# A masked softmax: SyncE waits for a ScalarE half tile before its first store

## Chip, cores, metric

One core of a Trainium2 chip. The metric is the device time in microseconds (us). All runs used here are at a granted clock of 1.0.

## The reference

```python
x: (16, 8, 256, 256) float32, lengths: 16 integers from 128 to 255
for b in range(16):
    masked = x[b, :, :, :lengths[b]]
    e = exp(masked - max(masked, axis=-1))
    result[b, :, :, :lengths[b]] = e / sum(e, axis=-1)     # the rest stays 0
```

The kernel leaves out the row maximum, which the drawn data allow. Every run reported here gave a correct result.

## The kernel before

A tile is one batch element: 2048 rows as 128 partitions x 16 rows x 256 columns, 2 MB. There are eight slots for tiles. SyncE loads tiles 0 to 3 whole and stores everything; GpSimd loads tiles 4 to 15, only as wide as the length asks; VectorE masks and divides; ScalarE computes exp and row sums, half a tile at a time.

```python
for h in range(2):                                   # SyncE: tile 0 in halves
    nc.sync.dma_start(out=xt[:, 0, s], in_=x_f[0, :, s]).then_inc(s_ld[h], 16)
for b in range(1, ahead):                            # tiles 1 to 3 (ahead = 4)
    nc.sync.dma_start(out=xt[:, b], in_=x_f[b]).then_inc(s_ld[b + 1], 16)
for b in range(batch):                               # stores
    s_b = s_st[b % 2]
    for s in parts(b):                               # tile 0: one part
        nc.sync.wait_ge(s_out, 2 * b + (s.stop - 1) // half + 1)
        if b >= 2 and s.start == 0:
            nc.sync.wait_ge(s_b, 64 * (b // 2 + 1))
        nc.sync.dma_start(out=out_f[b, :, s, :], in_=xt[:, b % slots, s, :]
            ).then_inc(s_b, 16 * ((s.stop - s.start) // quarter))
# ... GpSimd
nc.gpsimd.wait_ge(s_ld[ahead - 1], 16)               # tile 2 has landed
with nc.Fori(0, (batch - ahead) // 2, 1, engines=[POOL]) as q:
    # ... waits for the slot from the second round on, then the load of one tile
# ... VectorE: s_min counts masked halves, s_out divided halves
# ... ScalarE
with nc.Fori(0, 2 * batch, 1, engines=[ACT]) as i:
    nc.scalar.wait_ge(s_min, i + 1)
    for j in range(half):                            # 8 row groups
        ins = nc.scalar.activation(out=e, in_=e, func=EXP, accum_out=...)
    ins.then_inc(s_exp, 1)
```

The softmax here doesn't subtract the row's maximum and nothing guards it: scores larger than these inputs give would overflow.

## Time and profile before

| | before |
|---|---|
| time, median of 3 runs (range) | 156.89 us (156.85 to 157.22) |
| span of the profiled run | 155.3 us |
| bytes moved | 62.08 MB, 400 GB/s over the span |
| busiest engine | VectorE, 74% |
| first store issued | 18.86 us |
| tile 3 landed | 25.0 us |

The transfers bound the kernel: the page shows the DMA engines busy 0.9 or more in 38 of 40 slices, and DMA is 77% of the chain that ended last. The one stretch in which they run far below their usual rate, apart from the first and the last slice, is 20.5 to 25 us; it is called "the dip" below. The prediction shows the lines for it. Beside the views the text uses the trace's single records of DMA packets (queue, start, duration, size). Each transfer of SyncE leaves 16 records of 4 bytes (656 for the 41 transfers of the kernel before). Each is read here as the end of one of 16 parallel parts of SyncE's queue, and such a part is called a ring; that there are such parts is my reading of these records. A transfer is called "in the rings" from its issue to its landing. "Excess" is the time that packets took beyond the usual duration of their size, summed over the slower ones and divided by 16 engines. A slow stretch is said to begin when its first slow packet is overdue, that is at this packet's start plus the usual 0.61 us of a 16 KB packet.

### The profile page before, as it was taken

How to read it: one execution, taken by the hardware profiler on the slowest of the kernel's cores; microseconds unless marked ns; L12 is line 12 of the kernel's file. 1: busy time of each engine (PE TensorE's matmuls, PEld its weight loads, DVE VectorE, ACT ScalarE, POOL GpSimd, SP SyncE). 2: the span in 40 equal slices, each digit the busy share in tenths (PEclk: the TensorE clock that was granted, in tenths of full speed). 3: DMA queues.
4: the chain of work that ended last, by engine and by line, in shares of the span. 5: the costliest groups of instructions: out<-in, count | busy, mean ns of one | idle time of the engine just before them, and what ended most of it. 6: DMA issues, size and time to landing. Idle time of an engine off the chain costs nothing.

```text
span 155.3 us, 1316 instructions
## 1 busy us (share of the span) xinstructions
PE 0.2 (0%) x1; PEld 0.1 (0%) x1; DVE 115.6 (74%) x84; ACT 105.2 (68%) x514; POOL 19.0 (12%) x25
## 2 busy tenths in 40 slices
PE   0000000000000000000000000000000000000000
PEld 0000000000000000000000000000000000000000
DVE  1249999951999697997969696969698639796600
ACT  3087799992492978869595959596886906959100
POOL 4910031000220020200211020202000000000000
DMA  4999999999999999999999999999999999999991
GB/s 127 426 443 422 443 304 398 419 411 442 412 410 390 415 411 419 406 415 417 402 423 410 414 411 405 417 417 416 413 425 410 423 436 441 414 443 426 420 426 65
DMA packets 9988, 62.08 MB, mean 400 GB/s; under 512 B 850, under 2 KB 946, under 8 KB 6274
## 3 DMA queue, kind: packets, MB, share of 16 engines
q1 hardware_dynamic: 5904, 41.95, 65.7%
q0 software_dynamic: 4080, 20.12, 32.0%
q14 instruction: 2, 0.02, 0.0%
q10 hardware_dynamic: 2, 0.00, 0.0%
HBM read 28.51 MB, written 33.55 MB: 400 GB/s over the span
## 4 chain that ended last, share of the span: by engine, by line
DMA 77%; issue 7%; DVE 3%; ACT 3%; POOLq 3%; SPq 1%; ACTq 0%; POOL 0%; DVEq 0%
DMA xt<-in_x_dram 77%; ACT xt L252 3%; DVE xt L195 2%; DVE xt L222 1%; POOLq L99 1%; POOLq L135 1%; POOLq L130 1%; SPq L109 1%; ACTq L252 0%; POOL xt L130 0%; SPq L111 0%; POOLq L157 0%; DVE inv_sum L219 0%; POOLq L153 0%; POOLq L159 0%
## 5 line engine op out<-in xcount | busy, mean ns | idle before, releaser
L252 ACT ACTIVATE xt<-xt x256 | 102.4, 401 | 37.5 <-DVE xt L195 37.5
L222 DVE TENSOR_TENSOR xt<-xt,inv_sum 128x2048 f32<-128x2048 f32 x32 | 73.4, 2292 | 1.1
L252 ACT ACTIVATION_READ_ACCUMULATOR xt<-xt x256 | 47.8, 187 | 0.0
L195 DVE SCALAR_TENSOR_TENSOR xt<-down,len_s,xt 128x2048 f32<-128x2048 f32 (+1 forms) x17 | 37.8, 2222 | 13.3 <-DMA xt<-in_x_dram 13.2
L130 POOL DMA_DIRECT2D xt<-in_x_dram x12 | 12.8, 1064 | 95.6 <-issue 53.0
L219 DVE RECIPROCAL inv_sum<-row_sum 128x8 f32<-128x8 f32 x32 | 6.4, 199 | 14.4 <-ACT xt L252 14.4
L149 POOL MEMSET xt<- 128x1536 f32 x4 | 5.3, 1386 | 1.3 <-DVE len_s L186 1.3
L244 ACT ACT_TABLE_LOAD x1 | 1.3, 1283 | 1.6 <-SPq L79 1.6
L178 DVE TENSOR_SCALAR down<-iota_i 128x256 f32<-128x256 int32 x1 | 0.3, 298 | 1.6 <-POOL iota_i L141 1.6
L183 DVE CAST len_b<-word 1x16 bf16<-1x16 int32 x1 | 0.2, 161 | 0.5 <-DMA word<-in_lengths_dram 0.5
L186 DVE TENSOR_SCALAR len_s<-len_f 128x16 f32<-128x16 f32 x1 | 0.2, 175 | 0.4 <-PE len_f L165 0.4
L141 POOL IOTA iota_i<- 128x256 int32 x1 | 0.3, 332 | 0.6 <-SPq L79 0.6
L146 POOL MEMSET seed<- 1x1 f32 x2 | 0.3, 162 | 0.0
L244 ACT ACTIVATE warm<-const-float32-0.0 128x1 f32<-128x1 f32 x1 | 0.2, 203 | 0.0
L144 POOL MEMSET ones<- 1x128 bf16 x1 | 0.2, 194 | 0.0
L165 PE MATMUL len_f<-len_b,ones 1*128 1x16 bf16 x1 | 0.2, 168 | 2.8 <-DVE len_b L183 2.8
L270 POOL MEMSET const-float32-0.0<- 128x1 f32 x1 | 0.1, 98 | 0.3 <-issue 0.3
L165 PEld LDWEIGHTS len_f<-len_b,ones 1*128 1x128 bf16 x1 | 0.1, 97 | 2.7 <-POOL ones L144 2.7
L270 POOL MEMSET const-float32-1.0<- 128x1 f32 x1 | 0.1, 98 | 0.0
L270 POOL MEMSET const-bfloat16-1.0<- 128x1 bf16 x1 | 0.1, 98 | 0.0
L270 POOL MEMSET const-uint8-127<- 128x1 uint8 x1 | 0.1, 98 | 0.0
L270 POOL BASE_LOAD x1 | 0.0, 17 | 0.1
## 6 DMA issues: line engine op xcount, KB each, us to landing
out_dram<-xt SPq DMA_DIRECT2D x19, 1024.0 KB
out_dram<-xt SPq DMA_DIRECT2D x14, 512.0 KB
xt<-in_x_dram SPq DMA_DIRECT2D x3, 2048.0 KB, 16.2
out_dram<-xt SPq DMA_DIRECT2D x3, 2048.0 KB
xt<-in_x_dram POOLq DMA_DIRECT2D x3, 1728.0 KB, 17.0
xt<-in_x_dram POOLq DMA_DIRECT2D x2, 2048.0 KB, 18.9
xt<-in_x_dram POOLq DMA_DIRECT2D x2, 1600.0 KB, 17.2
xt<-in_x_dram POOLq DMA_DIRECT2D x2, 1280.0 KB, 14.5
```

The costliest lines, as they stand in the source:

```text
L99: return nc.values_load(at, engines=[engine], skip_runtime_bounds_check_because="compared with constants, never an address",)
L109: nc.sync.dma_start(out=xt[:, 0, s], in_=x_f[0, :, s]).then_inc(s_ld[h], 16)
L130: nc.gpsimd.dma_start(out=xt[:, slot, :, :w], in_=x_n[:, n, :, :w]).then_inc(s_sw[par], 16)
L135: with nc.gpsimd.If(v <= ws[m]):
L149: nc.gpsimd.memset(xt[:, b, :, low:], 0.0).then_inc(s_fill, 1)
L165: nc.tensor.matmul(len_f, lhsT=ones, rhs=len_b, start=True, stop=True).then_inc(s_lenf, 1)
L195: return nc.vector.scalar_tensor_tensor(out=t, in0=down[:, None, lo:hi].to_broadcast([P, s.stop - s.start, hi - lo]), scalar=len_s[:, b : ...
L219: step(nc.vector.reciprocal(out=inv_sum[:, b, s], in_=row_sum[:, b, s]))
L222: nc.vector.tensor_tensor(out=t, in0=t, in1=inv_sum[:, b, s, None].to_broadcast([P, half, seq_k]), op=ALU.mult,).then_inc(s_out, 1)
L244: nc.scalar.activation(out=warm, in_=nc.const_aps.tensor(0.0, (P, 1), F32), func=EXP)
L252: ins = nc.scalar.activation(out=e, in_=e, func=EXP, accum_out=sum_h[:, bass.ds(i, 1), j])
L270: nc = _bacc.Bacc("TRN2", target_bir_lowering=False, num_devices=1)
```

## The change

The first store is issued when tile 0 is divided, at 18.86 us, while tile 3's load is still in flight. The change holds it back until ScalarE has done the first half of tile 1, about a microsecond later. The intent, it seems, is to let tile 3's load pass undisturbed.

```diff
         for b in range(1, ahead):
             nc.sync.dma_start(out=xt[:, b], in_=x_f[b]).then_inc(s_ld[b + 1], 16)
+
+        nc.sync.wait_ge(s_exp, 3)
         for b in range(batch):
             s_b = s_st[b % 2]
```

## The prediction

> **What bounds the kernel now.** I read four views in this order: the page, the chain of waits of SyncE's queue, the busy time by stretches around the first store, and the timeline of single engines there. The page first.
>
> ```profile
> span 155.3 us, 1316 instructions
> PE 0.2 (0%) x1; PEld 0.1 (0%) x1; DVE 115.6 (74%) x84; ACT 105.2 (68%) x514; POOL 19.0 (12%) x25
> DMA  4999999999999999999999999999999999999991
> GB/s 127 426 443 422 443 304 398 419 411 442 412 410 390 415 411 419 406 415 417 402 423 410 414 411 405 417 417 416 413 425 410 423 436 441 414 443 426 420 426 65
> HBM read 28.51 MB, written 33.55 MB: 400 GB/s over the span
> DMA 77%; issue 7%; DVE 3%; ACT 3%; POOLq 3%; SPq 1%; ACTq 0%; POOL 0%; DVEq 0%
> ```
>
> The DMA line is 9 in every slice but the first and the last, and no compute engine is over 74% busy: the 62 MB of transfers bound this kernel (9988 packets, 62.08 MB by the page), and 77% of the chain that ended last is DMA. The GB/s line says how evenly: a first slice that starts empty, a last one that drains, some 390 to 443 between, and one exception, slice six (19.4 to 23.3 us) with 304. That slice is where the change acts, so I cut it up.
>
> ```profile
> 14.00:17.00 3.00, 0.00 (x0) 0.00 (x0) 2.97 (x4) 1.08 (x6) 0.00 (x0) 1.00 1.01 431
> 20.00:20.90 0.90, 0.00 (x0) 0.00 (x0) 0.90 (x1) 0.90 (x5) 0.00 (x0) 1.00 1.02 382
> 20.90:23.20 2.30, 0.00 (x0) 0.00 (x0) 2.27 (x3) 2.30 (x13) 1.30 (x1) 1.00 0.93 235
> 23.20:25.00 1.80, 0.00 (x0) 0.00 (x0) 1.77 (x3) 1.80 (x10) 0.56 (x1) 1.00 0.97 382
> 25.00:26.20 1.20, 0.00 (x0) 0.00 (x0) 1.20 (x2) 1.20 (x8) 0.00 (x0) 1.00 1.02 437
> ```
>
> The last two columns are the DMA share and GB/s. The share stays at 0.93 or more: the engines are not idle in the dip, their packets take longer. The single packet records of the trace agree: 16 KB packets take 611 ns each before and after, and 0.9 to 1.7 us between 20.9 and 23.2. The dip costs (431-235) x 2.3 us + (431-382) x 1.8 us + (431-382) x 0.9 us = 583 KB, at 431 GB/s 1.35 us. Adding up the excess of each packet over the usual time of its size gives 1.1 us. So about 1.1 to 1.35 us of the 156.9 are lost here. All other excess in the trace is 0.5 us at the very first packets.
>
> Now who does what around it, from the timelines of the single engines (start, duration):
>
> ```profile
> 18.86 26.07 SPq L118 DMA_DIRECT2D out_dram<-xt  x8
> 16.54 2.29 DVE L222 TENSOR_TENSOR xt<-xt,inv_sum 128x2048 f32<-128x2048 f32 x1
> 19.45 0.40 ACT L252 ACTIVATE xt<-xt  x1
> 19.76 0.19 ACT L252 ACTIVATION_READ_ACCUMULATOR xt<-xt  x1
> 20.94 1.30 POOL L130 DMA_DIRECT2D xt<-in_x_dram  x1 [12.42 <-issue]
> 24.29 0.56 POOL L130 DMA_DIRECT2D xt<-in_x_dram  x1 [2.05 <-issue]
> ```
>
> And when the early loads landed: a piece of the chain (start, duration; GpSimd's wait for tile 2 ends there), and the landing times of SyncE's three whole-tile loads.
>
> ```profile
> 2.51 16.19 DMA xt<-in_x_dram
> ...
> DMA to landing us min/median/max: 11.8/16.2/21.8
> ```
>
> The first store is issued at 18.86, right after VectorE ends tile 0's second division at 16.54 + 2.29 = 18.83. At that moment the loads of tiles 0 to 2 have just landed (2.51 + 16.19 = 18.70), and tile 3's 2 MB are in the rings: its load, issued last at 3.26, took 21.8 us to land, so it landed at 25.0.
>
> [...]the rings' end-of-transfer records for tile 3 lie at 23.2 to 24.7 us, the store's packets follow directly, and its issue had come 4.3 us before the first of them. [...]here GpSimd's packets first appear at 26.3, 5.3 us after its instruction. [...]undisturbed stretches here have 431[...].[...]
>
> **The change, part by part.** It adds one wait on SyncE, before the loop of stores, and removes nothing. Its count of 3 is reached when ScalarE ends the eighth row group of tile 1's first half: that activation starts at 19.45 and its accumulator is read from 19.76 for 0.19, so 19.95. With the 0.03 us that the store now takes from VectorE's end to issue, it goes in at about 19.98, against 18.86: 1.1 us later. The wait for VectorE has then been over for 1.1 us and costs nothing more.
>
> What does this delay touch? From issue (1.13) to its first packet record (2.14) the first load took 1.0 us[...]. The earliest ring is through with tile 3 at 23.2; without any dip it would be 23.2 - 1.0 = about 22.2. So 1.2 us of slack are left without the dip, and 2.2 with it: no ring runs dry. The bytes, the packet sizes, and the order (tile 3's load, store 0, store 1, GpSimd's loads beside them) are the same. The second store is issued at 23.75, when its own data are ready, over 3 us after the delayed first one, so SyncE doesn't pile up. Store 0 should land when it landed before, at about 31.7 us (the wait on it ends there), and so tile 2's store and GpSimd's reload of slot 0 keep their times. Sum: +1.1 us of issue, 0 us of path, 0 us of span. At the end SyncE still waits 6.4 us for stores alone, with the DMA at 401 to 434 GB/s up to 151: the last stores leave at the rate of the queue.
>
> **The rivals.**
> First, the early store causes the dip: [...]the delay lets more of tile 3 pass at full rate. For it: the dip stands between the first issue of a store and its first packet, and the change was presumably made for this. Against it: slowing begins at once on most engines, between 20.93 and 20.99, two us after the issue, and no later store issue shows such a thing (25.0 to 26.2 has 437, with a store issued at 23.75). If true, the dip shrinks or goes: up to 1.35 us less, 155.5 to 156.6.
> Second, GpSimd causes it: its first transfer instruction starts at 20.94, to 0.05 us where the packets begin to slow, and it is the longest of the twelve (1.30 against a median of 1.15). Against it: the other eleven leave no dip, so it would have to be a cost of the first one alone. GpSimd waits for tile 2's load, not for SyncE's store, so the dip stays and the time stays at 156.9. I hold this for likelier, 3 to 1.
> Third, the delay goes through in full: a bubble between tile 3 and store 0, or a later store 0 that holds slot 0 and GpSimd's reload. Then +1.1 us, 158.0. The slack of 2.2 us speaks against it.
> Fourth, the order between the two queues tips: with the store 1.1 us later, GpSimd's first packets might come in before part of store 0. They came at 26.3 and store 0 would have begun by 23.2 to 24.7, so only a dip that changes shape could do this; it would move tile 4 forward and store 0 back by well under 1 us, with the same bytes in all. Compute has room: ScalarE idles 37.5 us for VectorE, and VectorE 13.2 us for loads.
>
> **Range and chances.** Three parts in four for no change (156.9), one in four, less a little for the third rival, for a gain of around 0.6 to 1.2 us: the mean is 156.7 to 156.8, and I say 156.8. The three runs of before spread over 0.4 us. The low end is the first rival nearly whole, 155.9; the high end is half of the third plus spread, 157.5. A verdict of faster needs 3.1 us, more than twice the whole dip; slower needs 3.1 us too, nearly three times the delay. Faster 0.015, same 0.97, slower 0.015.
>
> **What would show each step.** In the changed profile the first store's issue should stand at 19.9 to 20.1. The GB/s line should again have one slice near 300 at 19.4 to 23.3, with the slow packets beginning at GpSimd's first transfer, about 20.9. Tile 3 should land at about 25.0 (21.8 us after issue), store 0 near 31.7, and GpSimd's second group of loads at the same places, 39.6 and 45.7 within half a us. If instead slice six is at 400 or more and tile 3 lands near 23.7, the first rival was right and the span is a microsecond shorter. If the DMA share drops below 0.9 near 23 us, there was a bubble after all. If the dip moves by 1.1 us with the store and keeps its size, the store causes it but the delay only shifts it. I would be wrong altogether if the time left 155.5 to 158.0: then something chaotic in the interleaving of the two queues is at work that I have not seen.

The forecast's sum came to +1.1 us of issue, 0 us of path and 0 us of span, from 156.9; with the rivals weighed in, to 156.8. No term of the sum is cut. What is cut are statements on the hardware that no trace or run of this case shows: in what order the rings and the queues are served, a highest rate (with the conclusion that nothing but the dip could be gained), a reason to suspect GpSimd, and what becomes of a store between its issue and its first packet. In place of the last: the slack of 1.2 and 2.2 us is 22.2 and 23.2 less 21.0. That 21.0, when the store is taken to be ready, is my estimate: the issue at 19.98 plus the 1.0 us that the first load took from issue (1.13) to first packet (2.14). The first rival uses the same 1.0 us: it has the store disturb the loads in flight when it arrives, about 1 us after 18.86.

## The result

| | before | changed |
|---|---|---|
| time, median of 4 runs each | 156.91 us (156.85 to 157.22) | 156.49 us (156.29 to 156.66) |
| ratio, 95% interval | | 0.9968 (0.9951 to 0.9986) |
| span of the profiled run | 155.3 us | 155.0 us |
| tile 3 landed | 25.0 us | 23.7 us |
| packet excess, 20 to 26 us | 1.11 us | 0.54 us |

A ratio is the mean time of one kernel's runs over that of the other's runs of the same rounds, so it is not quite the ratio of the medians. All outputs are right.

The page of the changed kernel, GB/s in 40 slices:

```profile
GB/s 110 427 457 410 440 376 422 401 408 440 412 409 392 403 410 420 409 415 414 407 422 406 419 405 411 415 412 424 410 420 412 428 439 427 412 450 423 395 425 85
```

Slice six has 376 in place of 304; the other slices are as before, within the scatter of a slice that holds only a few hundred packets.

The changed kernel by stretches (length, busy times of the engines, granted clock, DMA share, GB/s):

```profile
20.00:20.90 0.90, 0.00 (x0) 0.00 (x0) 0.90 (x1) 0.90 (x7) 0.17 (x1) 1.00 1.02 437
20.90:23.20 2.30, 0.00 (x0) 0.00 (x0) 2.27 (x3) 2.30 (x13) 1.12 (x1) 1.00 0.99 349
23.20:25.00 1.80, 0.00 (x0) 0.00 (x0) 1.77 (x3) 1.80 (x11) 0.56 (x1) 1.00 1.01 401
```

Against 382, 235 and 382 of before: the dip is about half as deep. The share of 0.99 to 1.02 shows no bubble for the later store.

The timeline of SyncE's queue in the changed kernel (start, duration of the merged row):

```profile
19.76 8.05 SPq L120 DMA_DIRECT2D out_dram<-xt  x4
```

Its timeline of GpSimd:

```profile
20.73 1.29 POOL L132 DMA_DIRECT2D xt<-in_x_dram  x1 [12.36 <-issue]
```

And the landing times of SyncE's three whole-tile loads in it:

```profile
DMA to landing us min/median/max: 11.5/16.0/20.5
```

The store is issued at 19.76. In this run everything on ScalarE stands 0.2 us earlier than in the run of before (the first activation of tile 1 starts at 16.43, not 16.64), so the delay that the wait makes is 1.1 us, as worked out. GpSimd's first transfer starts at 20.73. But by the packet records the first packet is overdue at 21.66, not at 20.7: the slow packets no longer begin where GpSimd begins. Tile 3, issued at 3.19, lands 20.5 us later, at 23.7. Two more signs moved that the prediction had unmoved: the slowest ring ends store 0 at 29.5 us in place of 31.2, and GpSimd's second group of loads starts at 38.55 and 44.71 in place of 39.57 and 45.74.

So the dip seemed to depend on the store, and the cause that the prediction preferred was in doubt at once.

### The profile page after: what moved, and what is told of

Its sections match the earlier page's. It is cut to its first block, busy times and chain, and to the rows that moved or that the text cites. A ratio compares the mean times of both kernels' runs of the same rounds, so it can differ in the third digit from the quotient of the medians.

```text
span 155.0 us, 1317 instructions
## 1 busy us (share of the span) xinstructions
PE 0.2 (0%) x1; PEld 0.1 (0%) x1; DVE 115.8 (75%) x84; ACT 105.2 (68%) x514; POOL 19.0 (12%) x25
## 4 chain that ended last, share of the span: by engine, by line
DMA 74%; DVE 6%; issue 6%; ACT 4%; POOLq 2%; SPq 1%; ACTq 1%; DVEq 0%
DMA xt<-in_x_dram 65%; DMA out_dram<-xt 10%; ACT xt L254 4%; DVE xt L197 3%; DVE xt L224 3%; ACTq L254 1%; SPq L109 1%; POOLq L132 0%; POOLq L137 0%; SPq L120 0%; POOLq L99 0%; DVE inv_sum L221 0%; SPq L111 0%; POOLq L159 0%; POOLq L155 0%
## 6 DMA issues: line engine op xcount, KB each, us to landing
xt<-in_x_dram POOLq DMA_DIRECT2D x2, 2048.0 KB, 18.5
```

## The experiments

**Theories.** *Store*: the first store, standing in the rings behind the loads, slows the packets ahead of it. *GpSimd*: its first transfer slows whatever is in flight. *Chance*: the gain of 0.3% is a difference between builds and nothing else.

### GpSimd moved away: e1_pool_after_tile3

```diff
-        nc.gpsimd.wait_ge(s_ld[ahead - 1], 16)
+        nc.gpsimd.wait_ge(s_ld[ahead], 16)
```

> The kernel before, with GpSimd waiting for tile 3's load instead of tile 2's before its first transfer, so that no GpSimd transfer is issued until about 24 us; the store stays at 18.9. If the early store makes the dip: still about 235 GB/s between 20.9 and 23.2, tile 3 lands near 25.0. If GpSimd's first transfer makes it: 420 GB/s or more there, tile 3 lands near 23.7, and whatever the first transfer costs comes after 24 us. The time itself may rise, since GpSimd's loads come some 4 to 5 us later: I expect 156.5 to 158 under either theory, so it is the stretch that decides.

157.73 us, 1.0055 of before (1.003 to 1.0081). The timeline of GpSimd in this run:

```profile
27.20 1.29 POOL L130 DMA_DIRECT2D xt<-in_x_dram  x1 [18.83 <-issue]
```

The dip's stretch in this run (columns as before):

```profile
20.50:23.50 3.00, 0.00 (x0) 0.00 (x0) 2.97 (x4) 3.00 (x16) 0.00 (x0) 1.00 0.97 289
```

The same stretch of the kernel before:

```profile
20.50:23.50 3.00, 0.00 (x0) 0.00 (x0) 2.97 (x3) 3.00 (x17) 1.30 (x1) 1.00 1.00 289
```

GpSimd does nothing between 20.5 and 23.5 (0.00 in the fifth column), its first transfer is 6.3 us later, and the rate is the same 289 GB/s. The first packet is overdue at 20.45, 1.8 us after the store's issue at 18.68. GpSimd is not needed for the dip. Its theory falls. The kernel got slower at its end: GpSimd's loads come later, and the last store is issued at 150.2 in place of 147.0.

### GpSimd earlier: e4_pool_early

```diff
-        nc.gpsimd.wait_ge(s_ld[ahead - 1], 16)
+        nc.gpsimd.wait_ge(s_ld[ahead - 2], 16)
```

> The kernel before, with GpSimd waiting for tile 1's load instead of tile 2's, so that its first transfer is issued near 16 us, 3 us before the first store. If GpSimd's first transfer makes the dip: slow packets from about 16 us, and none at 20.9. If the early store does: full rate at 16 to 18 and the dip about two us after the store's issue as before. Time 155.5 to 157.5: the same bytes, but tile 4 moves ahead of part of tile 3.

156.88 us, 1.0004 (0.998 to 1.0028). GpSimd's first transfer started at 15.98. The packets between 14 and 20 us have an excess of 0.06 us, those between 20 and 26 of 1.25. The stretch 20.5 to 23.5 has 314 GB/s, now with GpSimd's small packets, the first at 20.42, among the loads. The dip didn't move with GpSimd's instruction. As its packets lie in the dip here, the clean test is e1.

### No store in the rings until the loads have ended: e2_store_after_tile3

```diff
+        nc.sync.wait_ge(s_ld[ahead], 16)
         for b in range(batch):
```

> The kernel before, with SyncE waiting for tile 3's load to land before the first store is issued, so that no store is in the rings while loads are in flight. If the early store makes the dip: 420 GB/s or more until the loads end, which is then at about 22.2 to 23.2; tile 3 lands near 23.6, followed by a bubble of 1 to 1.5 us[...]. If GpSimd's first transfer makes it: packets slow down from about 20.9 all the same, tile 3 lands near 25.0, and then the bubble. Time: 156.5 to 157 under the first theory, 157.5 to 158.5 under the second.

157.95 us, 1.0082 (1.0059 to 1.0105). By stretches:

```profile
14.00:22.00 8.00, 0.00 (x0) 0.00 (x0) 7.82 (x7) 6.08 (x31) 1.11 (x1) 1.00 1.01 434
22.00:24.00 2.00, 0.00 (x0) 0.00 (x0) 1.97 (x3) 2.00 (x11) 0.74 (x2) 1.00 0.63 127
24.00:28.00 4.00, 0.00 (x0) 0.00 (x0) 4.00 (x2) 4.00 (x21) 0.00 (x0) 1.00 0.94 289
```

The timeline of SyncE's queue, with the first store:

```profile
23.71 1.22 SPq L119 DMA_DIRECT2D out_dram<-xt  x2
```

With no store behind them the loads run at 434 GB/s up to 22 us; by the packet records the rings finish tile 3 at 22.2 to 23.1 and not one of its packets takes over 700 ns, though GpSimd's first transfer started at 20.89. A gap follows (share 0.63). GpSimd's first packet comes at 22.89, and that of the store, issued at 23.71, only at 27.32. So from 23.1 until then all packets are GpSimd's, and many are slow in turn (excess 0.87 us between 20 and 26, 0.83 between 26 and 40), about 0.6 us of it before 24, when the store had hardly been issued. Here, then, the loads ahead were not slow without an early store, but the next stream started slowly without one. The store theory's mark is there; its time of 156.5 to 157 was wrong by a microsecond, probably because it had not allowed for GpSimd's slow packets beside the gap.

### The instruction without the delay: e3_wait_already_met, r2_wait_already_met

```diff
-        nc.sync.wait_ge(s_exp, 3)        # the changed kernel
+        nc.sync.wait_ge(s_exp, 2)
```

> The changed kernel with the count 2 in place of 3: the new wait is met at about 15 us, long before the wait for VectorE, so the instruction is there and the delay is not. Both theories of the dip say 156.9, first store at 18.9, the dip at 235 GB/s as before. If the gain of the change comes from the instruction itself or from chance of the build, this one shows it too, near 156.5.

157.19 us, 1.0033 (1.0008 to 1.0057). The store was issued at 18.98, and the stretch 20.5 to 23.5 has 289 GB/s: the full dip, as expected. But the time was 0.3% above before, not equal to it. That is as much as the change itself had gained, so single ratios of this size can't be taken for the effect. I ran both kernels again, on one chip:

> The control with count 2 again: the instruction without the delay. If the gain is the delay's, this one is 0.2 to 0.5 per cent slower than the changed kernel on the same chip, so 1.000 to 1.003 of before, with the full dip. If builds differ by chance only, no order between the two is expected.

> The changed kernel a third time, beside its control (next run) on one chip. Earlier: 0.9968 and 0.9987 of before. Expected 0.997 to 0.999, the dip again half as large as before (about 0.5 us of packet excess between 20 and 26 us against 1.0 to 1.1).

The changed kernel took 156.47 us, 0.9996 of before (0.9974 to 1.0017), the control 156.87, 1.0015 (0.9992 to 1.0037). The order is the one that the delay explains, but the two intervals against before overlap. Set against each other, six runs each, the control's mean is 0.36 us longer, with a 95% interval of 0.09 to 0.62 worked out from these twelve times. The dip's stretch in the control:

```profile
20.50:23.50 3.00, 0.00 (x0) 0.00 (x0) 2.97 (x3) 3.00 (x16) 1.30 (x1) 1.00 1.00 289
```

And in the changed kernel of the same chip:

```profile
20.50:23.50 3.00, 0.00 (x0) 0.00 (x0) 2.97 (x4) 3.00 (x16) 1.29 (x1) 1.00 0.98 377
```

### The changed kernel again: r1_after_again

> The changed kernel once more, on the chip of the three others. The first measurement gave 0.9968 of before, and a control that has the instruction but not the delay gave 1.0033 on another chip, so a difference of 0.3 per cent between builds may be nothing. Theory now held (the first store slows the packets in flight from about 2 us after its issue, and the delay halves that): the dip is half as deep as before again, store issued near 19.8, and 0.996 to 0.999 of the time before. If it was chance: 1.000 or above, with the same dip.

156.29 us, 0.9987 (0.9974 to 1.0001), excess 0.48 us, store at 19.79. In all three profiles of the changed kernel the excess between 20 and 26 us is 0.42 to 0.54; in the three with the early store (before and the two controls) 1.00 to 1.12. The halved dip is no chance. What reaches the time is smaller and less sure.

### Later still: e6_store_at_min6

```diff
-        nc.sync.wait_ge(s_exp, 3)        # the changed kernel
+        nc.sync.wait_ge(s_min, 6)
```

> The changed kernel, with SyncE waiting for VectorE's mask of tile 2 in place of ScalarE's half tile: the first store is issued at about 21.3, 1.5 us later still. If the store's start costs about a microsecond wherever it falls, slow packets when loads are in flight or a gap when they have ended: the loads end at full rate near 23.1, and a gap of 0.5 to 1.5 us follows; time at or above the changed kernel's, 0.998 to 1.004 of before. If later is simply better: 0.992 to 0.996.

157.14 us, 1.0039 (1.0026 to 1.0052). The timeline of SyncE's queue:

```profile
21.18 0.42 SPq L120 DMA_DIRECT2D out_dram<-xt  x1
```

By stretches:

```profile
14.00:22.00 8.00, 0.00 (x0) 0.00 (x0) 7.81 (x6) 6.08 (x31) 1.19 (x1) 1.00 1.01 432
22.00:24.00 2.00, 0.00 (x0) 0.00 (x0) 1.97 (x3) 2.00 (x12) 0.67 (x2) 1.00 0.94 340
...
23.50:29.00 5.50, 0.00 (x0) 0.00 (x0) 5.43 (x6) 5.50 (x29) 0.16 (x1) 1.00 0.97 349
```

The last of these stretches in the kernel before:

```profile
23.50:29.00 5.50, 0.00 (x0) 0.00 (x0) 5.43 (x6) 5.50 (x29) 0.56 (x1) 1.00 0.97 403
```

The loads are undisturbed to their end (22.2 to 22.9 by ring, 0.61 us a packet), although the store's packets follow them without a gap. Now the store's own packets are slow, the first of them overdue at 22.87, and the stretch after has 349 GB/s where before it had 403. Excess: 0.54 us between 20 and 26, 0.55 between 26 and 40, together as much as before. Later is not simply better: the changed kernel's delay stands between two costs.

### Is it the arrival of the store? e9_first_store_in_halves, e8_small_store_same_ring

In before, the controls, the changed kernel and e1 the first packet was overdue 1.8 to 2.1 us after the store's issue, and in e6 1.7 us after it, so its arrival in the rings could have been the cause. Two kernels put a store into the rings much earlier.

```diff
         if b == 0:
-            cuts = [0, nt]
+            cuts = [0, half, nt]          # e9: tile 0 stored in two halves
```

> The kernel before, with tile 0's store cut into two halves, so that a store of 1 MB is issued already at about 14.1 us, with 8 to 9 us of loads still ahead of it, and the second half at 18.9. If a waiting store slows the loads for as long as it waits: from about 16 to 23 us at 235 to 330 GB/s, some 2 to 3 us lost and the time up by as much. If the arrival alone costs: a dip of about 2 us from 16 on, full rate afterwards, time within 0.5 us of before. If the store slows only the last few packets ahead of it: the dip stays at 20.9 to 23.2 as before.

156.81 us, 1.0021 (0.9993 to 1.0049). SyncE's timeline:

```profile
14.01 0.42 SPq L118 DMA_DIRECT2D out_dram<-xt  x1
```

And the stretches:

```profile
15.50:18.50 3.00, 0.00 (x0) 0.00 (x0) 2.96 (x3) 1.97 (x10) 0.00 (x0) 1.00 1.02 437
18.50:20.50 2.00, 0.00 (x0) 0.00 (x0) 1.90 (x2) 2.00 (x12) 0.00 (x0) 1.00 1.02 426
...
20.50:23.50 3.00, 0.00 (x0) 0.00 (x0) 2.97 (x3) 3.00 (x17) 1.30 (x1) 1.00 0.96 273
```

A store of 1 MB was issued at 14.01, and nothing happened at 16: 437 GB/s. The dip came where it stands in the kernel before (273 GB/s, there 289), on the last two or three of each ring's eight packets of tile 3.

```diff
+        nc.sync.wait_ge(s_v, 1)           # e8, after the loads are issued
+        nc.sync.dma_start(out=out_f[batch - 1, :, 0, :], in_=down).then_inc(s_prime, 16)
```

SyncE waits for s_prime before tile 15's stores, which overwrite these rows.

> The kernel before, with a small store (128 rows of 1 KB) issued by SyncE right after its loads, at about 4 us, so that it waits in the loads' own rings until they end. If a store that waits in a ring slows the loads ahead of it for as long as it waits: 235 to 330 GB/s from about 6 us on and many microseconds lost. If only its arrival costs: a dip of 2 to 3 us at about 6, full rate from 9 to 20.9, then the dip of the large store as before or, if each ring pays once, none. If neither (the first large store alone does it): full rate from 6 to 20.9 and the dip as before. Time 0.3 us up in the last case, about 1 us up in the second.

157.16 us, 1.0039 (1.0011 to 1.0066). The small store was issued at 3.92 and stood in the rings for 19 us; 445 GB/s from 5.5 to 8.5, an excess of 0.02 us from 14 to 20, then 270 GB/s between 20.5 and 23.5. It is my third case, "neither": this store cost nothing where it arrived and nothing while it waited far behind. One caveat for both kernels: a further store is still issued at 18.7, as in the kernel before, so they show that arriving or waiting is not enough, and not that a late arrival plays no part.

### A small store on another queue: e5_early_small_store

The same store of 128 rows of 1 KB, issued by ScalarE after its table load (`nc.scalar.dma_start(...)`, again with s_prime).

> The kernel before, with one small store (128 rows of 1 KB, into rows of the last tile that are written over at the end) issued from ScalarE's queue at about 3.2 us. If the slow packets are a cost of the very first traffic towards the output, paid once: a small dip at about 5 us, none at 20.9 to 23.2 (420 GB/s or more there), tile 3 lands near 24.0, and up to 1 us less time than before, 0.994 to 0.999. If each first large store behind loads costs it, or each ring's first store: the dip stands at 20.9 to 23.2 as before, and the time is 0.3 us up.

156.74 us, 1.0029 (1.001 to 1.0049). The stretch 20.5 to 23.5 has 328 GB/s and an excess of 0.85 us between 20 and 26: still a dip. The first traffic to the output had long been done at 10 us, so the dip is not a price of that first traffic, paid once; a price that is paid more than once is not excluded by this run alone. The times of e5 and e8 rose by more than the 0.3 us of the extra bytes (an estimate, 131 KB at 431 GB/s): 0.45 and 0.6 us.

### A load that joins late: e7_late_load3

```diff
         for b in range(1, ahead):
+            if b == ahead - 1:
+                nc.sync.wait_ge(s_ld[2], 16)
             nc.sync.dma_start(out=xt[:, b], in_=x_f[b]).then_inc(s_ld[b + 1], 16)
```

> The kernel before, with tile 3's load issued only when tile 1 has landed (about 13.8 us) instead of at 3.3. If any transfer that joins a ring behind others in flight slows them two us later: a dip at about 15.8 to 18 as well. If it takes a store: full rate, 425 GB/s or more, from 14 to 20, and the dip at 20.9 as before. Time within 0.997 to 1.003 of before under the second, about 1 us more under the first.

157.06 us, 1.0039 (1.0022 to 1.0056). Tile 3's load was issued at 13.64; from 15.5 to 18.5 the rate is 431 GB/s, and the excess between 14 and 20 is 0.05 us. The dip stands at 20.5 to 23.5 with 289. A load that joined behind loads cost nothing here. The time went up 0.4%, though only the issue of one load was moved: one more sign that differences of 0.3 to 0.4% aren't to be read from one build.

## Why the prediction was right, and where its reasoning failed

**The size.** Predicted 156.8 us in 155.9 to 157.5, no change at 2%. Measured 156.49, and on later chips 156.29 and 156.47. The bound held, though that nothing but the dip could be gained was my estimate: its excess is 1.1 us, and all other excess in the trace is 0.5 us, at the very first packets. The forecast of no bubble held too (share 0.99 to 1.02). That the number held says little for the mechanism: the range was wide enough for most of the first rival's gain as well, and the point of 156.8 was a mean that leaned on the wrong cause.

**The delay.** Issue at 19.76 where 19.98 was worked out. The step is right; ScalarE stood 0.2 us earlier in that run.

**The weighing of the rivals failed.** The step "GpSimd waits for tile 2's load, not for SyncE's store, so the dip stays ... I hold this for likelier, 3 to 1" was wrong, and the first rival, which had one part in four, right in its main point. e1 shows it: the dip without GpSimd. With it fell "0 us of path": tile 3 and store 0 ended earlier. What misled me was the coincidence of GpSimd's start (20.94) and the first overdue packet (20.93). The controls have it again (20.99 and 21.04; 21.01 and 20.97). The trace holds a simple reason: the store was issued at 18.86 and tile 2, for which GpSimd waits, had landed at 18.70, so two us after the one is two us after the other. When the change moved the store, the slow packets went with it (21.66) and GpSimd did not (20.73). The argument "slowing begins at once on most engines, between 20.93 and 20.99" was a false reading besides. By 20.99 only two of the 16 rings had a packet overdue, while seven packets that started between 20.58 and 20.99 still took 0.61 us; and the first slow packet had started at 20.32, before GpSimd's instruction. "No later store issue shows such a thing" was true and no evidence: after tile 3 no SyncE load is ever ahead of a store again.

**The first rival's own mechanism is not shown either.** It had the store disturb the loads as it arrives, by my estimate about 1 us after the issue. e9 and e8 show that arriving is not enough: a store issued 4.9 or 14.9 us earlier slowed nothing when it would have come (437 and 445 GB/s). Two things stand in the runs. One is the place: of the loads mostly the last two or three 16 KB packets of each ring are slow, up to 1.7 us in the kernel before in place of 0.61, and in the changed kernel the last one or two, up to 1.2 us, so that the cost halves. The other is the time: with one store issued before the loads end (and e4 aside, where GpSimd's packets lie among them) the first packet is overdue 1.7 to 2.1 us after its issue, be that 18.68 (e1, e7) or 21.18 (e6); in e5, e8 and e9 it is 1.5 to 2.4 us after the issue of the store near 18.7 to 19.0. Place alone does not fit e6, where the store followed the loads at once and they went free; time alone does not fit the early stores of e8 and e9. Perhaps both are needed. A kernel that issues one store early and the next only after the loads have ended would tell; it was not run. If the store comes later still (e6, e2), the loads go free and what follows them costs as much or more. Whether a second passage from loads to stores in the same ring would cost it again stays open: this kernel has one passage only.

**Where the gain went.** Tile 3 ends earlier by 0.6 us: the mean of the 16 rings' end records is 22.9 to 23.0 us in the three profiles of the changed kernel, 23.5 to 23.6 in those of before and the controls. At the end of the kernel the slowest ring is ahead by 0.3 to 0.9 us (last packet 152.6 to 153.0 against 153.3 to 153.5), the mean of the rings by 0.0 to 0.4. Some is lost in the tail: the packet records of 130 to 152 us leave 0.14 to 0.27 us more idle time in the changed kernel, probably because the last stores have to wait for the computation of tile 15, which didn't come sooner (last store issued at 146.6 to 148.0, against 146.0 to 147.0). In time, three measurements give 0.9968, 0.9987 and 0.9996 of before. So the change gains between nothing and half a microsecond; the dip it halves would be worth 0.6.

No experiment beat the changed kernel.

## What to carry to other kernels

A loss in a saturated DMA stream can sit in slow packets, not in idle engines (235 GB/s at a DMA share of 0.93 in the kernel before): cut the time into stretches and compare GB/s with the share. Before trusting that two events coincide, ask what starts both, and move one of them; here a single changed semaphore index (e1) took GpSimd out of the question. And time a build against a control that carries the same instruction without its effect, since a control without the delay came out 0.3% above the kernel before here (e3, 1.0033; 1.0015 when it was run again).

## Two measurements beside

- Where loads passed to stores in SyncE's queue, the last 16 KB packets ahead of the first store took up to 1.7 us in place of 0.61 in the kernel before, and about 1.1 us were lost in all. No load packet took over 0.70 us where the store was issued after the loads (e2) or 1.0 us before the first ring had done with them (e6).
- GpSimd's first packet came 4.4 to 5.3 us after the instruction's start where SyncE's transfers filled the rings (e4, 15.98 to 20.42; before, 20.94 to 26.27), and 2.0 us after it in e2, where the loads in the rings ended at 22.2 to 23.1 (20.89 to 22.89). No run started one on idle rings.
